# Two small tiles move into the constants and one tile grows by 64 bytes: every later tile gets another start address

## The chip, the core and the metric

The kernel runs on one core of a Trainium2 chip. TensorE (PE in the profile) multiplies matrices, VectorE (DVE), ScalarE (ACT) and GpSimd (POOL) work element by element, and SyncE (SP) issues most of the DMA transfers. The metric is the device time of one execution in microseconds. Before the change the median of three runs is 1049.33 us, the lowest 1048.02 and the highest 1049.53.

## The reference, cut to what matters

The reference is a two-layer encoder on a sequence of 512 positions with 1024 features, in float32. Layer 0 mixes positions with stick-breaking attention of 16 heads, layer 1 with a gated linear recurrence; each layer ends in an MLP of width 4096 with a squared ReLU, and a last RMS norm stands at the end.

```python
def reference(x, norm_mix, norm_mlp, ...):
    for layer in range(2):
        h = rms_norm(x, norm_mix[layer])
        y = stick_breaking_attention(h, ...) if layer == 0 else rglru_block(h, ...)
        x = x + y
        h = rms_norm(x, norm_mlp[layer])
        u = relu(h @ w1)
        x = x + (u * u) @ w2
    return rms_norm(x, norm_final)
```

Nearly all the arithmetic is in dense products of a 512 x 1024 activation with weight matrices.

## The kernel before, in words

**Matrix products.** A float32 operand is split into a high half and a low half of type fp32r (`xgh` and `xgl` for the activations, `wh` and `wl` for the weights), and a product is three matmuls: high with high, high with low, low with high (`three`, L217). Each matmul has a stationary operand of 128 x 128, loaded by a weight load ahead of it, and a moving operand of 128 rows by 512, 384 or 256 columns that is streamed past it. ScalarE makes the high halves with a cast, VectorE the low halves with a subtraction.

**The MLPs.** Each MLP (class `Mlp`, one object for each layer) goes through the 4096 hidden features in four quarters. Its products are done with a Strassen-like scheme of seven block products. In the *up* products (`up`, L966) a 256-column half of the activations moves past weights: blocks 0, 1, 2 and 6 take it from `xgh`/`xgl`, blocks 4 and 5 from the tile `s41` (in the profile `s`) and the tiles `low`, block 3 from spare columns of `bh`/`bl` and `low`. In the *down* products (`times`, L1061) 512 columns of weights (`wh`, `wl`) move past the hidden activations, which lie in `bh`/`bl` (the first unit of a quarter) or in `sh`/`sl` (the second). The recurrence of layer 1 and the output projections use `dense` (L219 to L221), where `xgh`/`xgl` or `bh`/`bl` move past weights.

**What sets the order.** TensorE's order is the order of the program text; the order on the other engines is set by a scheduler together with chains of instructions held in sequence. None of it is touched here.

**What sets the addresses.** A tile pool takes a stretch of the on-chip memory (224 KiB in each of 128 partitions, the same address in all), and pools opened later lie behind the earlier ones. Every tile's length is rounded up to 32 bytes. The first pool is `const` (L89), and its small tile `eps_t` takes 32 bytes, so that `xgh`, the next large tile, starts at 2592, which is 32 more than a multiple of 256. All pools behind it inherit such a start. In layer 1's MLP a pool `last` of one tile each of 4, 48 and 16 bytes (L1584, L1611, L1613, L1614) stands ahead of the MLP's pools, so that these lie 128 bytes further on than in layer 0. `ss` and `bias` hold row sums of squares for the last norm; `early` is one element that nobody reads, written to have a table of ScalarE loaded in time.

Of the kernel before, what the change touches and what calls it, by code (L numbers as in the profile page):

```python
# [11 lines left out]
F32 = mybir.dt.float32  # L12
F32R = mybir.dt.float32r
AF = mybir.ActivationFunctionType
# [3 lines left out]
P = 128  # L18
S = 512
D = 1024  # L20
C = D // P
# [3 lines left out]
EPS = 1e-6  # L25
RG_C = 8.0
SCALE = HD ** -0.5


START = [  # L30
# [31 lines left out]
def hybrid_encoder(  # L62
# [24 lines left out]
    V, A, G, PE = nc.vector, nc.scalar, nc.gpsimd, nc.tensor  # L87

    const = ctx.enter_context(tc.tile_pool(name="const", bufs=1))  # L89
# [26 lines left out]
    make_identity(nc, ident)  # L116
    eps_t = const.tile([P, 1], F32, tag="eps", name="eps_t")
    V.memset(eps_t, EPS)

    xgh = const.tile([P, C, S], F32R, tag="xgh", name="xgh")  # L120
    xgl = const.tile([P, C, S], F32R, tag="xgl", name="xgl")
# [19 lines left out]
    class Squares:  # L141


        def __init__(self):
            self.acc = work.tile([P, S], F32, tag="ssq", name="ssq", bufs=1)
            self.begun = False
# [132 lines left out]
    NB = S // P  # L279
    PAIRS = H // 2  # L280
    half = [slice(0, HD), slice(HD, P)]
    so, early = {}, {}
# [7 lines left out]
    with ExitStack() as actx:  # L290
# [18 lines left out]
        for i in range(2):  # L309
            both = []  # L310
            for nm in ("h", "l"):
                t = sp.tile([P, 2 * P], F32R, tag=f"last{nm}{i}", name=f"last{nm}{i}")
# [120 lines left out]
        def inverse():  # L433
# [9 lines left out]
            with tc.high_priority():  # L443
                norm["root"] = A.activation(rc, pc[:, :NB], AF.Sqrt, bias=eps_t, scale=1.0 / D)
                V.reciprocal(rc, rc)
                for t in range(NB):
                    ts = slice(t * P, (t + 1) * P)
                    V.tensor_scalar(diag[:, ts], ident, rc[:, t : t + 1], None, ALU.mult)
                V.tensor_scalar(rp, rc, SCALE, None, ALU.mult)
                V.tensor_scalar(rn, rc, -SCALE, None, ALU.mult)  # L450
            norm.update(rc=rc, rp=rp, rn=rn)
# [315 lines left out]
    class Mlp:  # L767
# [28 lines left out]
        def __init__(self, ctx, layer):  # L796
            self.layer, self.sq, self.first = layer, Squares(), None
            self.V, self.A = Ordered(V), Ordered(A)
            self.mp = ctx.enter_context(tc.tile_pool(name=f"mlp{layer}", bufs=2))
            self.c = [  # L800
                self.mp.tile([P, 2, S], F32, tag=f"c{i}", name=f"c{i}", bufs=1) for i in range(4)
            ]
            self.begun, self.a = set(), {}
            self.turns = count()
            self.blocks = ExitStack()
            self.bp = self.blocks.enter_context(tc.tile_pool(name=f"blocks{layer}", bufs=2))
            self.u, self.lows, self.s3, self.slots = {}, {}, [], None

            self.s41 = self.bp.tile([P, C // 2, S], F32R, tag="s41", name="s41", bufs=1)

        def y(self, t, h):

# [500 lines left out]
    with ExitStack() as mctx:  # L1313
        mlp = Mlp(mctx, 0)
# [4 lines left out]
        last = {}  # L1319
# [261 lines left out]


    with ExitStack() as mctx:
        lp = mctx.enter_context(tc.tile_pool(name="last", bufs=1))  # L1584
        mlp = Mlp(mctx, 1)

        def between(c):
# [20 lines left out]
                )  # L1608


        A.activation(lp.tile([P, 1], F32, tag="rt", name="early"), eps_t, AF.Sqrt)  # L1611

        ss = lp.tile([P, NB, 3], F32, tag="ss", name="ss")  # L1613
        bias = lp.tile([P, NB], F32, tag="bias", name="bias")  # L1614

        def square(t, h, i, cols=slice(0, S), end=False):

# [129 lines left out]
```

## Time and profile before

| | |
|---|---|
| median of 3 runs | 1049.33 us (1048.02 to 1049.53) |
| span of the profiled execution | 1047.9 us |
| TensorE matmuls | busy 1035.1 us, 5868 |
| VectorE | busy 863.1 us, 1147 instructions |
| ScalarE | busy 701.5 us, 1082 instructions |
| mean granted TensorE clock | 0.996 |

The profiled execution shows its span, from the first to the last instruction, and no other time of its own; the median lies 1.4 us above it, and that difference is taken here for what lies around a span. Matmuls overlap in the records: a matmul's own duration holds the time until its last column has left the array, so what one costs in a long stream is the distance from its start to the next one's start. That distance is read from the view in order of time, whose rows give a start in microseconds, a duration, the engine, the line, output<-inputs and the shape.

### The profile page before, as it was taken

The numbers are of one execution on the slowest core, as the hardware profiler recorded it, in microseconds if no ns is written. First come the engines' busy times: TensorE is split into PE (matmuls) and PEld (weight loads), VectorE is DVE, ScalarE is ACT, GpSimd is POOL, SyncE is SP. The second block draws the span as 40 slices with busy tenths as digits, with TensorE's granted clock in tenths as the row PEclk, the third lists the DMA queues.
The fourth block names the chain that finished last, engine by engine and source line by source line (L and its number), as shares of the span: only waits on it lengthen the run. The fifth ranks groups of instructions, "written<-read, shape, count | busy, mean of one in ns | idle before, by whom it ended". The sixth has DMA issues, their size and how long they took to land.

```text
span 1047.9 us, 15859 instructions
## 1 busy us (share of the span) xinstructions
PE 1035.1 (99%) x5868; PEld 902.8 (86%) x5868; DVE 863.1 (82%) x1147; ACT 701.5 (67%) x1082; POOL 179.2 (17%) x238
## 2 busy tenths in 40 slices
PE   8999999999999999999999999999999999999997
PEld 7888888888888988988988788888888988988986
DVE  7888787848788898898899799984789797897897
ACT  6767676836766773773775699964755773773775
POOL 2344344420000010010011121200000010010013
PEclk9999999999999999999999999999999999999999
DMA  6745354537536667567582483352345667567553
GB/s 225 204 137 141 101 149 104 153 109 274 149 80 190 181 139 204 165 140 207 164 208 81 109 214 112 91 221 93 88 86 173 174 142 206 158 139 204 145 125 101
DMA packets 52828, 159.41 MB, mean 152 GB/s; under 512 B 6672, under 2 KB 7952, under 8 KB 52752
## 3 DMA queue, kind: packets, MB, share of 16 engines
q1 hardware_dynamic: 41808, 120.13, 34.4%
q0 software_dynamic: 10368, 37.75, 20.9%
q8 instruction: 46, 0.75, 0.3%
q10 hardware_dynamic: 576, 0.52, 0.2%
q14 instruction: 30, 0.25, 0.1%
HBM read 137.41 MB, written 4.19 MB: 135 GB/s over the span
## 4 chain that ended last, share of the span: by engine, by line
PE 88%; DVE 5%; ACT 3%; issue 2%; DMA 2%; ACTq 0%; POOL 0%; DVEq 0%; POOLq 0%
PE ps_t L1061 14%; PE ps_acc L966 8%; PE ps_z L966 8%; PE ps_acc L1061 7%; PE ps_acc L219 5%; PE ps_acc L221 5%; PE ps_acc L220 5%; PE ps_o L966 5%; PE ps_z L1061 4%; PE ps_o L219 2%; PE ps_t L220 2%; PE ps_o L220 2%; PE ps_o L221 2%; PE ps_t L221 2%; PE ps_t L219 2%
## 5 line engine op out<-in xcount | busy, mean ns | idle before, releaser
L757 ACT CAST wh<-b 128x1024 fp32r<-128x1024 f32 x168 | 174.0, 1047 | 125.6 <-DVE b L757 76.7
L757 DVE TENSOR_TENSOR wl<-b,wh 128x1024 fp32r<-128x1024 f32 x168 | 203.8, 1221 | 50.5 <-ACT wh L757 50.1
L1043 POOL DMA_DIRECT2D b<-in_w_dn x40 | 35.0, 875 | 360.9 <-DVE b L757 204.6
L219 PE MATMUL ps_acc<-xgh,wh 128*128 128x512 f32 x192 | 78.5, 409 | 0.0
L221 PE MATMUL ps_acc<-xgl,wh 128*128 128x512 f32 x192 | 75.2, 392 | 0.0
L220 PE MATMUL ps_acc<-xgh,wl 128*128 128x512 f32 x192 | 75.1, 391 | 0.0
L581 DVE TENSOR_TENSOR_SCAN scan<-keep,later 128x128 f32<-128x128 f32 (+1 forms) x64 | 59.6, 933 | 18.8 <-ACT keep L571 10.9
L214 DVE TENSOR_TENSOR wl<-raw,wh 128x512 fp32r<-128x512 f32 (+2 forms) x70 | 60.9, 895 | 16.2 <-ACT wh L212 16.1
L757 ACT ACTIVATE u<-u 128x512 f32<-128x512 f32 x100 | 63.1, 632 | 6.5 <-DVE u L757 4.8
L212 ACT CAST wh<-raw 128x512 fp32r<-128x512 f32 (+2 forms) x70 | 50.8, 759 | 23.1 <-PE ps_acc L221 7.3
L1043 POOL DMA_DIRECT2D b<-in_w_up x24 | 20.8, 867 | 240.5 <-DVE b L757 72.1
L585 POOL TENSOR_TENSOR w<-w,scan 128x128 f32<-128x128 f32 (+1 forms) x64 | 51.9, 813 | 55.9 <-DVE scan L581 53.2
L757 DVE TENSOR_TENSOR b<-b,b 128x1024 f32<-128x1024 f32 x48 | 58.7, 1224 | 1.3
L757 DVE TENSOR_TENSOR u<-u 128x512 f32<-128x512 f32 (+1 forms) x92 | 54.9, 596 | 2.7 <-ACT u L757 1.1
L966 PE MATMUL ps_z<-xgh,wh 128*128 128x256 f32 x192 | 54.2, 282 | 0.0
L966 PE MATMUL ps_z<-xgh,wl 128*128 128x256 f32 x192 | 54.1, 282 | 0.0
L757 ACT CAST wh<-raw 128x1024 fp32r<-128x1024 f32 x46 | 47.9, 1045 | 9.3 <-PE ps_acc L1061 8.4
L966 PE MATMUL ps_acc<-low,wh 128*128 128x256 f32 x192 | 53.6, 279 | 0.0
L1061 PE MATMUL ps_t<-wl,sh 128*128 128x512 f32 x126 | 50.1, 398 | 0.0
L1061 PE MATMUL ps_t<-wh,sh 128*128 128x512 f32 x126 | 49.6, 394 | 0.0
L1061 PE MATMUL ps_t<-wh,sl 128*128 128x512 f32 x126 | 49.4, 392 | 0.0
L1061 PE MATMUL ps_t<-wh,bh 128*128 128x512 f32 x126 | 49.2, 391 | 0.0
(399 smaller groups left out, 3434.4 us busy)
## 6 DMA issues: line engine op xcount, KB each, us to landing
b<-in_w_dn SPq DMA_DIRECT2D x48, 512.0 KB, 4.5
b<-in_w_dn POOLq DMA_DIRECT2D x40, 512.0 KB, 5.5
b<-in_w_up SPq DMA_DIRECT2D x36, 512.0 KB, 4.6
b<-in_w_up POOLq DMA_DIRECT2D x24, 512.0 KB, 5.3
raw<-in_w_m SPq DMA_DIRECT2D x16, 512.0 KB, 4.1
raw<-in_w_dn SPq DMA_DIRECT2D x16, 512.0 KB, 4.7
raw<-in_w_in SPq DMA_DIRECT2D x16, 512.0 KB, 4.2
raw<-in_w_qk SPq DMA_DIRECT2D x12, 512.0 KB, 3.7
```

The costliest lines, as they stand in the source:

```text
L212: A.copy(wh[:, k, :], raw[:, k, :])
L214: V.tensor_tensor(wl[:, k, :], raw[:, k, :], f(wh[:, k, :]), ALU.subtract)
L219: PE.matmul(ps, wh, ah, start=start, stop=False)
L220: PE.matmul(ps, wl, ah, start=False, stop=False)
L221: PE.matmul(ps, wh, al, start=False, stop=stop)
L581: V.tensor_tensor_scan(sc[:, S - n : S][:, ::-1], keep[:, :n][:, ::-1], later[:, S - n :][:, ::-1], 1.0, ALU.mult, ALU.max,)
L585: G.tensor_tensor(wt, wt, sc[:, S - n + 1 : S + 1], ALU.mult)
L757: ins = getattr(self.e, name)(*args, **kwargs)
L966: PE.matmul(ps[:, i * HS : (i + 1) * HS], m, y, start=new and i == k == n == 0, stop=i == 1 and k == C // 2 - 1 and n == 2, skip_group_che ...
L1043: G.dma_start(out=unit[b].rearrange("p j n -> p (j n)"), in_=unit["src"](to), accum_op=ALU.add)
L1061: PE.matmul(ps, m, y[:, jj, cols], start=first and n == 0, stop=last and n == 2, skip_group_check=not new,)
```

## The change

The last layer's pool is dropped. `ss` and `bias` become tiles of `const`, right behind `eps_t` and ahead of `xgh`; they take 64 and 32 bytes, so `xgh` and everything behind it move by 96 bytes. The one-element write `early` now goes to the first column of the MLP's result tile `c[0]`, which is overwritten later. And `s41`, the first tile of the pool of an MLP's blocks, gets 16 more elements (64 bytes) at its end that nobody uses, so that the blocks of weights behind it and `sh`/`sl` move by another 64 bytes. All engines execute the same instructions in the same order on the same amounts of data; the single ScalarE instruction `early` has another output and waits for two more semaphores.

```diff
+ASIDE = 16
...
     eps_t = const.tile([P, 1], F32, tag="eps", name="eps_t")
     V.memset(eps_t, EPS)
+    ss = const.tile([P, S // P, 3], F32, tag="ss", name="ss")
+    bias = const.tile([P, S // P], F32, tag="bias", name="bias")
...
-            self.s41 = self.bp.tile([P, C // 2, S], F32R, tag="s41", name="s41", bufs=1)
+            t = self.bp.tile([P, C // 2 * S + ASIDE], F32R, tag="s41", name="s41", bufs=1)
+            self.s41 = t[:, : C // 2 * S].rearrange("p (k s) -> p k s", s=S)
...
-        lp = mctx.enter_context(tc.tile_pool(name="last", bufs=1))
         mlp = Mlp(mctx, 1)
...
-        A.activation(lp.tile([P, 1], F32, tag="rt", name="early"), eps_t, AF.Sqrt)
-
-        ss = lp.tile([P, NB, 3], F32, tag="ss", name="ss")
-        bias = lp.tile([P, NB], F32, tag="bias", name="bias")
+        A.activation(mlp.c[0][:, 0, :1], eps_t, AF.Sqrt)
```

The built programs tell where the operands lie. The table lists all 5596 fp32r matmuls by the start address of the moving and of the stationary operand, as the rest of a division by 256 bytes; the text calls this rest the *residue* of an operand.

| columns | moving, stationary (where) | matmuls | residues before | residues after |
|---|---|---|---|---|
| 512 | `xg`, `bh`/`bl` past `wh`/`wl`, or `wh`/`wl` past `bh`/`bl` | 2016 | 32, 32 | 128, 128 |
| 256 | `xg`, `bh`/`bl` past `wh`/`wl` (up products), weights of v past `xg` | 1644 | 32, 32 | 128, 128 |
| 256 | `s41`, `low` past `wh`/`wl` | 552 | 224, 32 | 64, 128 |
| 256 | layer 1: `s41` and one `low` past `wh`/`wl` | 216 | 96, 32 | 64, 128 |
| 512 | `wh`/`wl` past `sh`/`sl`, layer 0 | 336 | 32, 224 | 128, 128 |
| 512 and 256 | `wh`/`wl` past `sh`/`sl`, layer 1 | 330 and 12 | 32, 96 | 128, 128 |
| 512 | recurrence and end of attention, weights in other pools | 234 | 32, 224 | 128, 64 |
| 256 to 512 | attention scores and values | 224 | 224, 224 | 64, 64 |
| 256 | last block of attention values (`last`) | 32 | 64, 224 | 160, 64 |

So before the change every moving operand but `last` starts 32 bytes off a multiple of 64, and every stationary one does; after it all but those 32 start on a multiple of 64, and 4338 matmuls have both operands on a multiple of 128.

## The prediction

> **What bounds the kernel now.** I read the page first, then who waits for whom on TensorE, then the matmuls in order of time, then the busy time by stage.
>
> ```profile
> PE 1035.1 (99%) x5868; PEld 902.8 (86%) x5868; DVE 863.1 (82%) x1147; ACT 701.5 (67%) x1082; POOL 179.2 (17%) x238
> PEclk9999999999999999999999999999999999999999
> PE 88%; DVE 5%; ACT 3%; issue 2%; DMA 2%; ACTq 0%; POOL 0%; DVEq 0%; POOLq 0%
> ```
>
> ```profile
> PE ps_z L437 <- DVE ssq L422: 1.6, 1, 1.6
> PE ps_z L381 <- DVE eps_t L118: 1.1, 1, 1.1
> PE ps_z L966 <- ACT u L757: 1.0, 1, 1.0
> PE ps_t L220 <- DVE wl L757: 0.8, 1, 0.8
> ```
>
> TensorE is busy 99% of the span at full clock, 88% of the chain that ended last is its own, and the four longest waits it has for others add up to 4.5 us. So the time is the number of matmuls times the distance from one to the next, and the question is whether that distance depends on where operands lie.
>
> **What a matmul costs at which placement.** Each pair of rows is the first and the last of a stretch without a gap in which all matmuls have one shape and, but for the parts of the last pair that are named below, one placement.
>
> ```profile
> 250.38 0.39 PE L219 MATMUL ps_o<-xgh,wh 128*128 128x512 f32 x1
> ...
> 288.24 0.39 PE L221 MATMUL ps_z<-xgl,wh 128*128 128x512 f32 x1
> ```
>
> 512 columns, residues 32 and 32: 167 steps in 37.86 us, 226.7 ns each.
>
> ```profile
> 333.65 0.28 PE L966 MATMUL ps_acc<-xgl,wh 128*128 128x256 f32 x1
> ...
> 336.17 0.28 PE L966 MATMUL ps_acc<-xgl,wh 128*128 128x256 f32 x1
> ...
> 336.88 0.28 PE L966 MATMUL ps_acc<-low,wh 128*128 128x256 f32 x1
> ...
> 338.92 0.28 PE L966 MATMUL ps_acc<-low,wh 128*128 128x256 f32 x1
> ```
>
> 256 columns: at residues 32 and 32, 21 steps in 2.52 us, 120.0 ns each; at 224 and 32, 18 steps in 2.04 us, 113.3 ns each. Same shape, same kind of weights, half a microsecond apart, and 6.7 ns less.
>
> ```profile
> 322.46 0.39 PE L1061 MATMUL ps_t<-wh,sh 128*128 128x512 f32 x1
> ...
> 327.95 0.39 PE L1061 MATMUL ps_t<-wh,bh 128*128 128x512 f32 x1
> ...
> 791.65 0.40 PE L1061 MATMUL ps_t<-wh,sh 128*128 128x512 f32 x1
> ...
> 797.25 0.39 PE L1061 MATMUL ps_t<-wh,bh 128*128 128x512 f32 x1
> ...
> 805.67 0.28 PE L966 MATMUL ps_acc<-s,wh 128*128 128x256 f32 x1
> ...
> 808.38 0.28 PE L966 MATMUL ps_acc<-low,wh 128*128 128x256 f32 x1
> ```
>
> The same program lines in layer 0 and layer 1, which differ only in the 128 bytes of the pool `last`: the 24 `sh`/`sl` matmuls take 228.8 ns each in layer 0 (residues 32 and 224; 5.49 us) and 233.3 in layer 1 (32 and 96; 5.60 us); the 256-column stretch that took 113.3 ns in layer 0 takes 117.8 in layer 1 (23 steps in 2.71 us; `s` at residue 96, most `low` still at 224). The placement sets part of the distance.
>
> From 256 to 512 columns at one placement the distance grows by 106.7 ns, that is 0.417 ns for a column, so 512 columns need 213.3 and 256 need 106.7. What remains is a fixed part: 13.3 ns at residues 32 and 32, 6.7 at 224 and 32, 15.5 at 32 and 224, 20.0 at 32 and 96. The 6.7 is 16 columns, or 64 bytes of an operand's row, and the 13.3 is twice that. This looks like rows read in pieces of 64 bytes: an operand that starts in the middle of a piece touches one piece more than its length needs.
>
> **The change, part by part.**
>
> The tiles themselves. No instruction is added or removed. `early` keeps its place on ScalarE (0.19 us at 693.74) and waits for two semaphores more, GpSimd's and its own engine's:
>
> ```profile
> 693.74 0.19 ACT L1611 ACTIVATE early<-eps_t 128x1 f32<-128x1 f32 x1
> 681.51 0.92 POOL L1530 TENSOR_SCALAR aa<-d 128x512 f32<-128x512 f32 x1 [8.59 <-DVE d L757]
> ```
>
> GpSimd's last piece of work ahead of it ended at 682.4, 11 us earlier. Behind `early` on ScalarE stands a cast into `xgh`; if this cover were gone, that cast and the MLP's first matmuls would be late by the difference. I cost it at nothing.
>
> VectorE and ScalarE. Their tiles move too. The trace has one operation at several placements:
>
> ```profile
> L757 DVE TENSOR_TENSOR wl<-b,wh 128x1024 fp32r<-128x1024 f32 x168 | 203.8, 1221 | 50.5 <-ACT wh L757 50.1
> L757 DVE TENSOR_TENSOR b<-b,b 128x1024 f32<-128x1024 f32 x48 | 58.7, 1224 | 1.3
> L757 DVE TENSOR_TENSOR wl<-raw,wh 128x1024 fp32r<-128x1024 f32 x38 | 46.7, 1229 | 1.1 <-ACT wh L757 1.0
> ```
>
> `b` lies at residues 224 and 96, `raw` at 32, most of `wh` and `wl` at 32: 1221, 1224 and 1229 ns, within 0.7%. I take nothing for these engines.
>
> The one placement for both layers. The two dearest placements disappear: layer 1's 342 `sh`/`sl` matmuls go from 20.0 ns of fixed part to that of two equal residues (now 13.3), 342 x 6.7 = 2.3 us; layer 0's 336 from 15.5, 0.7 us; some 288 of layer 1's up products (two blocks in two units in three quarters, 24 each) from 117.8 to 113.3, 1.3 us. Together 4.3 us, and this much follows even if only the difference of the two residues counts, since everything else keeps its difference (64 - 128 is 224 - 32 less a whole 256). The quarters say the same: layer 0's second up product starts 77.94 us after its first, layer 1's third 78.68 after its second.
>
> ```profile
> 333.42 0.28 PE L966 MATMUL ps_acc<-xgh,wh 128*128 128x256 f32 x1
> ...
> 411.36 0.28 PE L966 MATMUL ps_acc<-xgh,wh 128*128 128x256 f32 x1
> ...
> 883.01 0.28 PE L966 MATMUL ps_acc<-xgh,wh 128*128 128x256 f32 x1
> ...
> 961.69 0.28 PE L966 MATMUL ps_acc<-xgh,wh 128*128 128x256 f32 x1
> ```
>
> The start on a multiple of 64. No fp32r matmul of the trace has both operands there, so its price is bounded. Upper end: the whole 13.3 ns goes (6.7 where only that is left). Lower end: nothing goes, or the fixed part rises to the largest one seen, 20.0. I take one piece of 64 bytes, 6.7 ns a matmul, which is the smallest step between the rows and the one by which the 113.3 and the 120.0 differ: 5596 x 6.67 = 37.3 us. With the 4.3 that is 41.6 us of TensorE's time.
>
> The rule in the Trainium skill, TensorE: Matmul & The Clock Gate, section "Wait — 56ns, not 53.3ns?", is that a warm stream of matmuls runs at its columns over 2.4 GHz plus a fixed 2.5 ns or so. The trace's 0.417 ns for a column agrees, its fixed 6.7 to 20 ns does not; by that rule some 10 ns could go from each matmul, an estimate of about 60 us of TensorE's time.
>
> What the other engines let through. The stages of the down products are the narrow ones:
>
> ```profile
> 360.00:411.00 51.00, 51.00 (x278) 44.07 (x278) 48.61 (x55) 30.48 (x39) 5.20 (x6) 1.00 0.69 182
> ...
> 575.00:690.00 115.00, 114.01 (x498) 93.04 (x497) 99.64 (x142) 100.31 (x138) 20.41 (x18) 1.00 0.46 124
> ...
> 860.00:882.00 22.00, 22.00 (x96) 17.70 (x95) 21.34 (x24) 9.77 (x11) 1.73 (x2) 1.00 0.72 209
> ```
>
> (Stretch, its length, then busy time and instructions of TensorE, weight loads, VectorE, ScalarE, GpSimd.) In the first, TensorE's 278 matmuls lose 1.85 us and come to 49.15, while VectorE has 48.61 of work and idles 2.4 us now, mostly behind ScalarE's casts (50.1 of the 50.5 us of idle time in the `wl` row). If half of that idle time stays, the stage ends at 49.8 and gives 1.2 instead of 1.85. There are seven such stages, 4.5 us given back. In the third, 0.64 us would bring TensorE to 21.36 and VectorE is at 21.34. The recurrence (second row) keeps 11 us of room. The start and the end of the kernel, where little is streamed, cost another 2.5. So 41.6 - 7 = 34.6 us come through. The span of 1047.9 with 1.4 around it is the median, 1049.3; 1049.3 - 34.6 = 1014.7, say 1015. What is late next is VectorE's subtraction into `wl` in the down stages.
>
> **The rivals.**
>
> *All of the fixed part goes.* For it: it is 16 or 32 columns, pieces of 64 bytes, and both operands are now aligned. Against it: the tiles `last` start on a multiple of 64 as moving operands (their stationary ones do not) and are no faster than others of 256 columns:
>
> ```profile
> 119.19 0.28 PE L629 MATMUL ps_o<-lasth,v 128*128 128x256 f32 x1
> 119.31 0.28 PE L630 MATMUL ps_o<-lastl,v 128*128 128x256 f32 x1
> 119.43 0.28 PE L478 MATMUL ps_acc<-wh,xgh 128*128 128x256 f32 x1
> ```
>
> Two of them take 0.24 us. Price: 5596 x 13.3 less 768 x 6.6 is 69.3, with the 4.3 73.6 us; VectorE's floors in the seven stages keep some 12 of it: 988. Chance 0.24.
>
> *Only the difference of residues counts.* Then 13.3 ns is what a change of weights costs, and only the 4.3 us come: 1045. For it: the two layers, at one and the same 32 bytes off, already differ by 6.7 ns. Against it: the fixed part comes in steps of 64 bytes of row. Chance 0.20.
>
> *Placement does nothing that counts.* A matmul reads its rows in small pieces of which all these starts are multiples, the layers differ for another reason, and the time stays within 0.2%, which is about what a measurement of this kernel can tell from no change. Chance 0.07. The Trainium skill, SBUF — State Buffer, section "Specifications (TRN2)", gives pieces of 16 bytes, by which this would hold, as every start is a multiple of 32 before and after; the 113.3 against 120.0 speaks against it.
>
> *Equal residues collide.* This is the one on the other side. If the moving and the stationary stream get in each other's way when both start at the same place of a 256-byte stretch, and the more so the more exactly they start together, then the 4338 matmuls at 128 and 128 rise to the dearest fixed part seen, 20.0: 4338 x 6.7 = 28.9 us, all of it paid, since TensorE bounds: 1078. It decides from the point at which the 256-column `xg` stretch takes more than 120 ns a step. For it: 224 and 32 is cheaper than 32 and 32. Against it: 32 and 96 is dearer than 32 and 32. Chance 0.13.
>
> **How the numbers follow.** One piece less at each matmul: 0.36, 1015 us, by itself 1005 to 1025 (what VectorE gives back). With 0.24 for 988, 0.20 for 1045, 0.07 for no change and 0.13 for 1078, faster by over 0.2% is 0.36 + 0.24 + 0.20, less a little for a 1045 that half fails: 0.79; same 0.08; slower 0.13. The range from 985 to 1049 leaves out the collision (0.13) and what of the cheapest case lies still lower (978 to 998 by itself, some 0.07).
>
> **What would show it.** In the view in order of time the 256-column `xg` stretch of an up product goes from 120.0 to about 113 ns a step and the 512-column stretch from 226.7 to about 220; a step of 107 and 213 would be the first rival, 120 and 226.7 unchanged the second. Layer 1's quarter should equal layer 0's. VectorE's busy time should stay at 863 us and its share rise to 85%, with waits of TensorE for `wl` in the down stages. I am wrong if the steps stay, or if they shrink and the waits take more than 7 us back.

## The result and the profile after

The changed kernel takes 1048.23 us in the median of 13 runs (1045.75 to 1049.71), the kernel before 1049.07 us beside it (1048.02 to 1051.06). The ratio of the two is 0.9981 with a 95% interval of 0.9972 to 0.9989: 2.0 us shorter, between 1.2 and 2.9; the two medians alone are 0.8 us apart. The forecast was 1015. The profiled execution took 1046.34 us, with a span of 1044.4, 3.5 less than before. It is one of the shorter ones: the median of the 13 spans is 1046.3. In the later runs of both kernels an execution takes 1.9 us more than its own span, where 1.4 was taken ahead of the prediction; the gain that was forecast does not rest on it.

From the page of the changed kernel, the engines and the chain that ended last:

```profile
PE 1030.6 (99%) x5868; PEld 901.4 (86%) x5868; DVE 862.3 (83%) x1147; ACT 701.5 (67%) x1082; POOL 180.4 (17%) x238
PE 84%; DVE 7%; ACT 4%; issue 3%; DMA 2%; POOL 0%; ACTq 0%; SPq 0%; DVEq 0%; POOLq 0%
```

TensorE is busy 4.5 us less and its part of the chain fell from 88% to 84%, while VectorE's rose from 5% to 7% and ScalarE's from 3% to 4%. VectorE's own work is unchanged.

The matmuls of the changed kernel in order of time, each pair being the first of a stretch and the first behind it or the last of it, at the places that the prediction read, and for the last pair one quarter later:

```profile
250.61 0.39 PE L222 MATMUL ps_o<-xgh,wh 128*128 128x512 f32 x1
...
288.46 0.39 PE L224 MATMUL ps_z<-xgl,wh 128*128 128x512 f32 x1
...
322.61 0.39 PE L1065 MATMUL ps_t<-wh,sh 128*128 128x512 f32 x1
...
328.05 0.39 PE L1065 MATMUL ps_t<-wh,bh 128*128 128x512 f32 x1
...
333.60 0.28 PE L970 MATMUL ps_acc<-xgh,wl 128*128 128x256 f32 x1
...
336.12 0.28 PE L970 MATMUL ps_acc<-xgh,wl 128*128 128x256 f32 x1
...
789.99 0.39 PE L1065 MATMUL ps_t<-wh,sh 128*128 128x512 f32 x1
...
795.43 0.39 PE L1065 MATMUL ps_t<-wh,bh 128*128 128x512 f32 x1
...
884.08 0.29 PE L970 MATMUL ps_acc<-s,wh 128*128 128x256 f32 x1
...
886.81 0.28 PE L970 MATMUL ps_acc<-bh,wh 128*128 128x256 f32 x1
```

512 columns at residues 128 and 128: 167 steps in 37.85 us, 226.7 ns, as at 32 and 32 before. 256 columns at 128 and 128: 21 steps in 2.52 us, 120.0 ns, as before. So the move of all these operands to multiples of 64 bought nothing. What did change are the streams that had another placement in the two layers: 24 `sh`/`sl` steps take 5.44 us in layer 0 and in layer 1, 226.7 ns each (228.8 and 233.3 before), and 24 steps of `s`/`low` in layer 1 take 2.73 us, 113.8 ns (117.8 at the same place before).

The starts of the up products show it by quarters (to be read with 333.49 for the first of layer 0):

```profile
411.38 0.28 PE L970 MATMUL ps_acc<-xgh,wh 128*128 128x256 f32 x1
...
489.25 0.28 PE L970 MATMUL ps_acc<-xgh,wh 128*128 128x256 f32 x1
...
800.87 0.28 PE L970 MATMUL ps_acc<-xgh,wh 128*128 128x256 f32 x1
...
881.20 0.28 PE L970 MATMUL ps_acc<-xgh,wh 128*128 128x256 f32 x1
...
959.07 0.28 PE L970 MATMUL ps_acc<-xgh,wh 128*128 128x256 f32 x1
```

Layer 1's second step is 959.07 - 881.20 = 77.87 us (78.68 before), the same as layer 0's 489.25 - 411.38 = 77.87. Its first step is 80.33, and before it was 883.01 - 802.79 = 80.22: there nothing came through. The waits of TensorE in the changed kernel from 735 us on (between 235 and 575 us none is long enough to be listed), and three places in order of time:

```profile
PE ps_z L970 <- ACT u L760: 1.2, 1, 1.2
PE ps_acc L970 <- ACT u L760: 0.4, 1, 0.4
PE ps_t L1065 <- DVE wl L760: 0.2, 1, 0.2
```

```profile
389.30 0.39 PE L1065 MATMUL ps_t<-wh,sh 128*128 128x512 f32 x1
389.70 0.50 PE L1065 MATMUL ps_t<-wl,sh 128*128 128x512 f32 x1
390.04 0.39 PE L1065 MATMUL ps_t<-wh,sl 128*128 128x512 f32 x1
...
806.39 0.28 PE L970 MATMUL ps_acc<-low,wh 128*128 128x256 f32 x1
807.05 0.38 PE L970 MATMUL ps_acc<-bh,wh 128*128 128x256 f32 x1 [0.38 <-ACT u L760]
...
858.99 0.39 PE L1065 MATMUL ps_t<-wh,sh 128*128 128x512 f32 x1
859.54 0.50 PE L1065 MATMUL ps_t<-wl,sh 128*128 128x512 f32 x1 [0.16 <-DVE wl L760]
```

The third place in the kernel before:

```profile
860.65 0.40 PE L1061 MATMUL ps_t<-wh,sh 128*128 128x512 f32 x1
860.89 0.50 PE L1061 MATMUL ps_t<-wl,sh 128*128 128x512 f32 x1
```

Each wait is short, some below what the view of waits lists, but each takes a few tenths. From the first row to the second it is 0.40 us at 389.30 (0.28 before, 0.23 without a wait) and 0.55 at 858.99 (0.24 before), where TensorE is ready too early for VectorE's `wl`; at 806.39 it is 0.66 (0.12 before), where it is ready too early for ScalarE's result.

To add all this up, the matmul rows of two profiles were put beside each other in program order and the distances from each start to the next subtracted. A distance of more than 30 ns over the columns at 2.4 GHz in either profile counts as a wait, the others as stream. For the two MLPs (235 to 575 us, and 735 us to the end):

| pair of profiles | streams, us | waits, us | sum, us |
|---|---|---|---|
| before to after | -4.3 | +1.7 | -2.6 |

Of the 4.3, 2.0 are layer 1's `sh`/`sl`, 0.7 layer 0's, 1.0 the `s`/`low` streams, 0.5 the `bh`/`bl` matmuls of the down products. 1.2 of the 1.7 us of waits lie between 802 and 960 us. Outside the MLPs the same sums give 0.2 us more before 235 us and 1.2 less in the recurrence, where two waits differ (588.46 and 589.72 before: 1.9 us for two distances; 0.7 now). These two places also differ, by up to 2.9 us, between profiles of kernels whose edits touch neither, and in the two further pairs with this same change, below, the recurrence differs by 0.0 and 0.1 us. So they are taken to be no part of the change.

### The profile page after: what moved, and what is told of

Its sections match the earlier page's. It is cut to its first block, busy times and chain, and to the rows that moved or that the text cites. A ratio compares the mean times of both kernels' runs of the same rounds, so it can differ in the third digit from the quotient of the medians.

```text
span 1044.4 us, 15859 instructions
## 1 busy us (share of the span) xinstructions
PE 1030.6 (99%) x5868; PEld 901.4 (86%) x5868; DVE 862.3 (83%) x1147; ACT 701.5 (67%) x1082; POOL 180.4 (17%) x238
## 4 chain that ended last, share of the span: by engine, by line
PE 84%; DVE 7%; ACT 4%; issue 3%; DMA 2%; POOL 0%; ACTq 0%; SPq 0%; DVEq 0%; POOLq 0%
PE ps_t L1065 13%; PE ps_acc L970 8%; PE ps_z L970 7%; PE ps_acc L1065 7%; PE ps_acc L222 4%; PE ps_acc L223 4%; PE ps_acc L224 4%; PE ps_o L970 4%; PE ps_z L1065 3%; DVE wl L760 2%; PE ps_o L222 2%; PE ps_t L223 2%; PE ps_t L224 2%; PE ps_t L222 2%; PE ps_o L223 2%
## 5 line engine op out<-in xcount | busy, mean ns | idle before, releaser
L760 DVE TENSOR_TENSOR wl<-b,wh 128x1024 fp32r<-128x1024 f32 x168 | 203.6, 1220 | 49.2 <-ACT wh L760 48.9
L760 DVE TENSOR_TENSOR b<-b,b 128x1024 f32<-128x1024 f32 x48 | 58.7, 1223 | 1.3
L1065 PE MATMUL ps_t<-wl,bh 128*128 128x512 f32 x126 | 49.1, 390 | 0.0
```

The source lines that it names most:

```text
L760: ins = getattr(self.e, name)(*args, **kwargs)
L1065: PE.matmul(ps, m, y[:, jj, cols], start=first and n == 0, stop=last and n == 2, skip_group_check=not new,)
```

## The experiments

**Streams alone.** Is it where the operands start, or how far apart? A kernel of nothing but streams of 36 matmuls in the pattern of `three`, with the moving and the stationary operand at chosen starts:

```python
for n, kind in ((512, "wide"), (256, "half")):
    for i in range(16):
        stream(f"{kind}_move_{L[i]}", n, 32 * i, 0)       # moving at 0, 32, 64, ... bytes
    for i in range(8):
        stream(f"{kind}_both_{L[i]}", n, 32 * i, 32 * i)  # both
    for i in range(8):
        stream(f"{kind}_stat_{L[i]}", n, 0, 32 * i)       # stationary
```

> This kernel computes nothing of the reference; it only streams fp32r matmuls, 36 in a row for each placement, with stationary operands at a fixed residue and moving operands at residues 0, 32, ... 480 (names move), both at the same residue 0 to 224 (both), moving at 0 and stationary at 0 to 224 (stat), and moving 4 or 16 bytes on (fine), for 512 and for 256 columns. Theory A (the distance depends on moving residue minus stationary residue alone): all eight 'both' streams take 226.7 and 120.0 ns a matmul; 'move' at 192 (that is 224 and 32) takes 113.3 at 256 columns, at 64 (96 and 32) 117.8; 'stat' at 192 (32 and 224) takes 228.9 at 512 columns and at 64 (32 and 96) 233.3; 'move' repeats itself after 256 bytes, and some differences not yet seen, such as 128, may be cheaper or dearer than all of these. Theory B (rows are read in pieces of 64 bytes and the start itself counts): 'both' at 0, 64, 128 and 192 is cheaper by 6.7 ns than at 32, 96, 160 and 224.

In the view in order of time each stream is one row, so the distance of two rows' starts is that of 36 matmuls and one change of the output bank:

```profile
35.68 8.57 PE L44 MATMUL wide_move_b<-mv,st 128*128 128x512 f32 x36
44.08 8.41 PE L44 MATMUL wide_move_c<-mv,st 128*128 128x512 f32 x36
52.34 8.57 PE L44 MATMUL wide_move_d<-mv,st 128*128 128x512 f32 x36
...
169.44 8.36 PE L44 MATMUL wide_both_b<-mv,st 128*128 128x512 f32 x36
177.63 8.36 PE L44 MATMUL wide_both_c<-mv,st 128*128 128x512 f32 x36
185.82 8.36 PE L44 MATMUL wide_both_d<-mv,st 128*128 128x512 f32 x36
...
382.66 4.47 PE L44 MATMUL half_both_b<-mv,st 128*128 128x256 f32 x36
386.97 4.47 PE L44 MATMUL half_both_c<-mv,st 128*128 128x256 f32 x36
```

Both at 32 take 8.19 us (`both_b`), both at 64 take 8.19 (`both_c`), and so do all eight: with equal residues the absolute start does not matter. Moving 32 ahead takes 8.40, 64 ahead 8.26. Inside the streams, with d for moving less stationary start mod 256 bytes, a 512-column matmul takes 226.7 ns at d = 0, 228.9 at 64, and 232.7 to 234.5 at 32, 96, 128, 160, 192 and 224; it repeats after 256 bytes, and the stationary side mirrors the moving one. 256 columns take 120.0 at d = 0 and 116.7 to 120.0 at the others, but at 192 either 113.3 or 117.8. This settles the kernel's rows: 32 past 224 before was d = 64 (228.8 in both), 32 past 96 was d = 192 (233.3 in both), `s`/`low` at 224 past 32 was 192 (113.3) and at 96 past 32 was 64 (117.8), and equal residues are 226.7 and 120.0 wherever they are.

**Without the padding.** The changed kernel without its 64 bytes: `sh`/`sl` fall back to d = 64, in both layers.

```diff
-ASIDE = 16
+ASIDE = 0
```

> The changed kernel without the 64 bytes behind s41: sh/sl lie at 64 instead of 128, with wh/wl at 128. Theory A: both layers' sh/sl matmuls take the 228.9 ns of layer 0 before instead of 226.7; 678 of them cost 1.5 us, so this is 0.5 to 1.5 us slower than the changed kernel and 0.5 to 2 us faster than the kernel before, whose layer 1 had the dearer placements; layer 1's s/low matmuls stay at 113.5. Theory B': the gain is not from placement but from run to run differences of waits at the start and between the layers: then this run cannot be told from the changed kernel, and sh/sl still take 226.7.

1047.83 us, 0.9991 (0.9982 to 0.9999) of the kernel before, which took 1048.8 us beside it. By the ratios that is 1.0 us more than the changed kernel, as expected, but the two intervals overlap. The distances decide. The 24 `sh`/`sl` steps again, in layer 0:

```profile
323.06 0.39 PE L1065 MATMUL ps_t<-wh,sh 128*128 128x512 f32 x1
...
328.55 0.39 PE L1065 MATMUL ps_t<-wh,bh 128*128 128x512 f32 x1
```

5.49 us, 228.8 ns a step, with both operands on a multiple of 64. All `sh`/`sl` together take 1.25 us more than with the padding. So of the 4.3 us the pool `last`, whose 128 bytes set the layers apart, is worth 3, the padding 1.25.

**All starts 32 bytes on.** One tile of 32 bytes ahead of `xgh` takes every large tile off the multiples of 64, with all differences kept.

```diff
+    const.tile([P, 8], F32, tag="aside", name="aside")
```

> The changed kernel with 32 unused bytes ahead of xgh: every difference of residues is that of the changed kernel, but no large tile starts on a multiple of 64 any more (160 and 160 instead of 128 and 128). Theory A: every stream takes what it takes in the changed kernel (226.7, 120.0, 113.5), and the time is the changed kernel's within 0.1%, 0.998 of the kernel before. Theory B: matmuls get dearer and the time is at or above that of the kernel before.

1047.5 us, 0.9986 (0.9978 to 0.9995); the streams differ from the changed kernel's by 0.2 us in sum. The absolute start is worth nothing in the whole kernel either. The profiled execution was the slowest of the twelve (1049.56 us), and in the MLPs it waits 2.3 us longer than the changed kernel's, most of it at one place:

```profile
830.51 0.51 PE L971 MATMUL ps_z<-bh,wh 128*128 128x256 f32 x1 [1.86 <-ACT u L761]
830.81 0.42 PE L971 MATMUL ps_z<-bh,wl 128*128 128x256 f32 x1
```

Behind this wait for ScalarE's `u`, of 1.2 us in the changed kernel, the granted clock is 0.50 for some 3 us and 256-column matmuls are 0.21 us apart. Since the streams agree and the twelve times do not show such a loss, it is taken for a difference between executions. It tells how far the waits of a single profile can be trusted.

**Differences made worse.** 128 bytes between `bl` and everything behind it, so that all products of `xg`, `bh` and `bl` with weights go from d = 0 to 128, still on multiples of 128:

```diff
+    const.tile([P, 32], F32, tag="aside", name="aside")
```

> The changed kernel with 128 unused bytes behind bl: xgh, xgl, bh and bl stay, all weights move by 128, so that moving and stationary operands lie 128 apart in 2016 matmuls of 512 columns and 1644 of 256. Theory A, priced by the streams measured alone (233.5 instead of 226.7 at 512 columns, 118.7 instead of 120.0 at 256; and 234 matmuls from 228.8 to 233.3): 13.7 - 2.1 + 1.1 = 12.7 us of TensorE's time, all paid since it bounds: about 1060 us, ratio to the kernel before 1.010. Rival C (TensorE's distances are not what sets the time, since the other engines' work has to fit beside it anyway): under 4 us more than the changed kernel.

1055.33 us, 1.0041 (1.0025 to 1.0058). The stretch that took 226.7 ns:

```profile
250.59 0.39 PE L224 MATMUL ps_o<-xgh,wl 128*128 128x512 f32 x1
...
289.15 0.40 PE L225 MATMUL ps_z<-xgl,wh 128*128 128x512 f32 x1
```

166 steps in 38.56 us, 232.3 ns. The streams take 10.1 us more than in the changed kernel, where 12.7 was forecast. The spans of the two profiled executions differ by 8.8 us, the times by 6.3 (from the two ratios, whose intervals leave 4 to 8), so the forecast ratio of 1.010 was missed and the rival's limit of 4 us was passed. The difference alone moves the time, and more than half of the loss on TensorE is paid. In layer 0's MLP the waits are 0.9 us shorter, since TensorE comes later to the halves that it waited for; in layer 1's they are 0.8 longer, with the clock halved for a while as in the run before.

**A cheaper difference for the up products.** Since 256 columns can take 113.3 ns at d = 192, the MLPs used `xg` 64 bytes lower against the weights.

```diff
-    xgh = const.tile([P, C, S], F32R, tag="xgh", name="xgh")
-    xgl = const.tile([P, C, S], F32R, tag="xgl", name="xgl")
+    def placed(name, more):
+        t = const.tile([P, C * S + more], F32R, tag=name, name=name)
+        return [t[:, o : o + C * S].rearrange("p (c s) -> p c s", s=S) for o in (ASIDE, 0)]
+
+    (xgh, uph), (xgl, upl) = placed("xgh", 4 * ASIDE), placed("xgl", ASIDE)
...
-                return xgh[:, c, ts], xgl[:, c, ts]
+                return uph[:, c, ts], upl[:, c, ts]
```

> The changed kernel with xgh and xgl lengthened, so that the MLPs use them 64 bytes lower than the attention and the recurrence do: moving less stationary residue is 192 instead of 0 for 1056 up matmuls of 256 columns and for 384 of 512 columns (the MLPs' first products). Theory A with the streams measured alone (113.3 instead of 120.0, 233.3 instead of 226.7): -7.0 + 2.5 = -4.5 us of TensorE's time against the changed kernel; if all comes through about 1043 us, ratio to the kernel before 0.994; if half is given back to waits as in the change itself, 0.996. If those streams fall into the other state that the same residues showed alone (117.8), -2.3 + 2.5: nothing gained. Rival C: no difference from the changed kernel.

1050.43 us, 0.9996 (0.9985 to 1.0006): no gain. The 512-column products went to 233.3 ns, and the up products took 117.2 to 118.0 in the mean instead of 113.3. The `s`/`low` streams, whose difference the edit leaves as it is, went from 114.1 and 115.8 ns to 117.3 and 118.0, so that the streams of the MLPs became 2.0 us longer than in the changed kernel.

**What picks 113.3 or 117.8.** Streams alone again, 72 matmuls of 256 columns at d = 192, made by the moving side 192 higher (`move`) or the stationary side 64 higher (`stat`), each behind another stream:

```python
lead = dict(wide=(512, 0, 0), half=(256, 0, 0), ahead=(256, 64, 0), odd=(256, 96, 0))
for i, (name, how) in enumerate(lead.items()):
    for kind, rm, rs in (("move", 192, 0), ("stat", 0, 64)):
        stream(f"lead_{L[i]}", *how)
        stream(f"{name}_then_{kind}", 256, rm, rs, reps=24)
```

> This kernel computes nothing of the reference. Streams of 72 matmuls of 256 columns at residues 192 and 0 (move) and at 0 and 64 (stat), each right behind 36 matmuls of another placement; then streams of 384 columns at differences 0, 64, 128 and 192. If the two values seen for one difference (113.3 and 117.8) are two states of which the start of the stream picks one, the value changes with what ran ahead, and both placements show both values. If it is the placement itself (residue 0 and 64 is not 192 and 0), 'move' always takes 113.3 and 'stat' always 117.8.

```profile
36.30 8.64 PE L44 MATMUL wide_then_move<-mv,st 128*128 128x256 f32 x72
44.78 8.32 PE L44 MATMUL lead_a<-mv,st 128*128 128x512 f32 x36
...
65.75 8.34 PE L44 MATMUL half_then_move<-mv,st 128*128 128x256 f32 x72
73.92 4.46 PE L44 MATMUL lead_b<-mv,st 128*128 128x256 f32 x36
```

The very same 72 matmuls take 8.48 us behind 512-column ones and 8.17 behind 256-column ones at d = 0, 117.8 and, once settled, 113.3 ns each. Behind 256-column ones at d = 64 or 96 `move` takes 8.48 again. `stat` takes 8.48 behind the first two and 8.17 and 8.18 behind these. One difference has two states; what runs ahead picks one, and it lasts. (384 columns took 173.4, 173.3, 175.9 and 176.8 ns at d = 0, 64, 128 and 192.)

**Why half came back: VectorE's sums left out.** TensorE's streams became 4.3 us shorter and the MLPs 2.6. If the rest went to waits for VectorE, it must come through when VectorE has less to do. The same edit in the kernel before and in the changed one:

```diff
             if far or name in self.FAR:
                 G.dma_start(
                     out=unit[b].rearrange("p j n -> p (j n)"), in_=unit["src"](to), accum_op=ALU.add
                 )
-            elif to:
-                self.V.tensor_tensor(unit[b], unit[b], unit[to], ALU.add)
```

> The kernel before, with VectorE's 48 sums of weight blocks (the b<-b,b group, 48 x 1.224 us = 58.7 us of VectorE in the two MLPs) left out; the products that would use those sums then use the plain block, so this part of the computation is wrong and only the time is read. It is one half of a pair with the run that follows. Theory A (placement gives TensorE 4.2 us, and in the MLPs it then waits for halves of weights that VectorE is late with, which gives half back): this kernel is itself only 0 to 2 us faster than the kernel before, since before TensorE waits for VectorE little, and its own small waits of about 1 us in the MLPs go. Theory B (the 2.0 us that are missing have nothing to do with VectorE): the same here, 0 to 1 us; the two theories part in the next run.

> The changed kernel with the same 48 sums left out (the same part of the computation wrong). Theory A: with 58.7 us less of work on VectorE its halves of weights are there in time, so the whole placement gain shows: 3.5 to 4.2 us below the run before this one, in place of the 2.0 us that the two full kernels are apart. Theory B (what comes back is waits for ScalarE's u at a quarter's start, or run-to-run waits elsewhere): the pair stays 1.5 to 2.5 us apart.

1047.75 us (0.9984, 0.9975 to 0.9993) and 1043.01 us (0.9937, 0.9924 to 0.9951): 4.7 us apart (4.9 by the ratios, 3.5 to 4.2 expected), against 2.0 with the sums. (The first of the two is 1.7 us below the kernel before, as theory A had it.) The distances say why: in the MLPs the streams of this pair differ by 4.7 us and the waits by 0.0; between 235 and 575 us and from 735 us on, the trace of the second kernel lists no wait of TensorE. The gain of the placement was whole all along, and VectorE's sums held about half of it back. Leaving them out takes work from VectorE and also a step out of the chain ahead of `wl`; this pair does not part the two, the sums on POOL below keep the step.

**More for TensorE to win.** With what the streams alone had shown, only the upper chunks of `xg` are put 192 bytes higher in the MLPs, so that their products follow 256-column ones with d = 0.

```diff
+    UP = 3 * ASIDE
+    def placed(name):
+        t = const.tile([P, C * S + 4 * ASIDE], F32R, tag=name, name=name)
+        return [t[:, o : o + C * S].rearrange("p (c s) -> p c s", s=S) for o in (0, UP)]
...
+        def __getitem__(self, at):
+            c = at[1].start if isinstance(at[1], slice) else at[1]
+            return (self.hi if c >= C // 2 else self.lo)[at]
```

> The changed kernel, with chunks 4 to 7 of x times the norm's gain kept 192 bytes higher by the MLPs (chunks 0 to 3 stay where they were; each of the two tiles has 256 bytes more, so everything behind keeps its residue). 576 of the 256-column products (P2 and P4) then stand at a difference of 192 and follow equal-residue 256-column streams (P7, P1); 192 of the 512-column ones stand at 192 as well. If the state of a stream is picked by what runs ahead of it, as in the streams measured alone (113.32 after a 256-column stream with equal residues, moving side 192 higher), the 576 gain 6.7 ns each = 3.8 us and the 192 lose 6.6 ns each = 1.3 us: 2.6 us less on TensorE than the changed kernel, of which 1 to 2.6 us show: 1045.6 to 1047.2 us beside 1048.2, a ratio to the kernel before of 0.9955 to 0.997. If waits between the streams let them fall to the other state (117.8), 576 x 2.2 = 1.3 us gained against 1.3 lost: no change from the changed kernel.

1048.61 us, 0.9999 (0.9989 to 1.0009). The 48 steps of upper chunks in an up product, and the waits for `wl` in the down products:

```profile
349.45 0.28 PE L987 MATMUL ps_z<-xgh,wh 128*128 128x256 f32 x1
...
354.89 0.28 PE L987 MATMUL ps_z<-xgh,wh 128*128 128x256 f32 x1
```

```profile
PE ps_t L1082 <- DVE wl L777: 1.2, 5, 0.3
```

113.3 ns a step, as hoped; the streams of the MLPs are 2.0 us shorter than in the changed kernel. But the waits there are 3.3 us longer, with five for `wl` where there was one. In these profiles TensorE's gain is not only lost: its waits cost more than it, which neither case of the expectation had. The same kernel with the sums left out:

> The kernel with the upper chunks of x 192 bytes higher, and VectorE's 48 sums of weight blocks (58.7 us) left out, so the products that use them are wrong and only the time is read. In the run of the former with the sums the MLPs' streams on TensorE became about 2.2 us shorter and its waits in the same stretches 3.4 us longer. Theory A (VectorE sets the pace there, and TensorE's gain turns into waits for it): without the sums the gain shows, 1.5 to 2.6 us below the changed kernel without the sums (1043.01): 1040.4 to 1041.5, a ratio of about 0.9915 to 0.9925 to the kernel before. Theory B (the waits come from the placement itself, or from the other engines' writing to the higher places): no lower than the changed kernel without the sums, 1043 to 1045.

1040.73 us, 0.9911 (0.9897 to 0.9925), 2.3 us below the changed kernel without the sums, with 2.7 us less of streams in the MLPs and no waits. Both placements pay in full as soon as VectorE is not late.

**The sum by DMA.** In a complete kernel, one more group of sums taken from VectorE: the second group of the down half's P6, whose `wl` is the one waited for at 389.3 us.

```diff
-            FARS = [("P6", 0)]
+            FARS = [("P6", 0), ("P6", 1)]
```

> The changed kernel, complete, with one more of the sums taken from VectorE: for the second group of the down half's P6 the DMA that loads the block adds it (as it does already for the first group), 8 x 1.224 = 9.8 us less on VectorE, 8 x 0.87 us more on POOL, 4 MB more to move. TensorE's small waits for wl in the down halves stand at this product (the wl needed at 389.3 us). Theory A: those waits go and a part of what came back shows: 0.5 to 1.5 us below the changed kernel, 1046.7 to 1047.7, a ratio of 0.9967 to 0.9976 to the kernel before. Against it: the DMA can start only when the product two steps ahead has its halves, some 5.6 us before they are needed, and such a transfer takes 5.6 us to land; if it is late, TensorE waits up to 1 us in each of 8 quarters: up to 1056.

> Both edits: upper chunks 192 bytes higher, and the DMA's sum for the second group of P6. Theory A: TensorE has 2.2 us less to do in the MLPs and VectorE 9.8 us less; 1 to 3 us below the changed kernel with the upper chunks higher alone (1048.6): 1045.6 to 1047.6, and no slower than the run before this one; a ratio of 0.996 to 0.998 to the kernel before. Theory B (waits come from elsewhere): within 1 us of 1048.6. If the transfer is late: as in the run before, above 1050.

1072.38 us (1.0218, 1.0203 to 1.0232) and 1073.26 us (1.0228, 1.0213 to 1.0242). Of the first, TensorE's two longest waits, one of them in order of time, and the granted clock (the eighth column) in a stretch behind it:

```profile
PE ps_t L1065 <- ACT wh L760: 8.9, 7, 1.4
PE ps_t L1065 <- DVE wl L760: 5.3, 7, 0.8
```

```profile
393.01 0.50 PE L1065 MATMUL ps_t<-wh,sh 128*128 128x512 f32 x1 [1.32 <-ACT wh L760]
394.27 0.80 PE L1065 MATMUL ps_t<-wl,sh 128*128 128x512 f32 x1 [0.76 <-DVE wl L760]
394.87 0.63 PE L1065 MATMUL ps_t<-wh,sl 128*128 128x512 f32 x1
395.30 0.63 PE L1065 MATMUL ps_t<-wh,sh 128*128 128x512 f32 x1
```

```profile
394.30:395.50 1.20, 1.20 (x3) 1.01 (x4) 1.20 (x2) 1.20 (x3) 0.87 (x1) 0.50 0.00 0
```

The transfer is late, the case that the expectation named as against it, but the price was put at up to 1 us a quarter. In this quarter it is 3.8 beside the changed kernel: 2.1 us of waiting, and behind it matmuls 427 ns apart at half the clock. Over the MLPs it is 23.9 us: 3.7 to 4.2 in the five quarters where the clock was halved, 2.6, 1.3 and 0.4 in the others. These two runs say nothing on VectorE.

**The sum on POOL.** POOL is nearly idle there (5.2 us of the 51 in the prediction's first stretch) and needs no transfer.

```diff
-            elif to:
-                self.V.tensor_tensor(unit[b], unit[b], unit[to], ALU.add)
+            elif to:
+                e = G if pool else self.V
+                e.tensor_tensor(unit[b], unit[b], unit[to], ALU.add)
...
-                if ahead > (5 if far else 2 if name == "P5" else what[0] == "up"):
+                pool = (*what[::2], name) == ("down", 1, "P6")
+                if ahead > (5 if far or pool else 2 if name == "P5" else what[0] == "up"):
```

> The changed kernel, complete, with the sum of weight blocks for the second group of the down half's P6 made by POOL instead of VectorE: 8 x 1.224 = 9.8 us less on VectorE. POOL's nearest rows are 128x512 sums of 1.29 to 1.7 us, so 2.6 to 3.4 us for one of 128x1024, which starts two steps (5.6 us) ahead of the halves that need it, where the DMA needed 0.87 + 5.6 us. Theory A (VectorE's load gives half of the gain back): the waits for wl of 0.1 to 0.5 us a quarter go, 0.5 to 1.5 us below the changed kernel: 1046.7 to 1047.7, a ratio of 0.9967 to 0.9976 to the kernel before. Theory B (VectorE's load does not matter in the complete kernel): within 0.4 us of the changed kernel. If POOL's sums slow VectorE beside them, or are late: slower than 1049.

> The same with the upper chunks of x 192 bytes higher in the MLPs, where TensorE has 2.2 us less to do. Theory A: more of it shows than without POOL's sums: 1 to 3 us below the 1048.6 of that kernel, 1045.6 to 1047.6, a ratio of 0.996 to 0.998. Theory B: within 1 us of 1048.6. Late or disturbed: above 1049.

1048.81 us (0.9994, 0.9982 to 1.0006) and 1049.24 us (1.0005, 0.9996 to 1.0014): neither shows a gain in the time, and the range of theory A was missed by both. By distances against the changed kernel, the first lost 1.1 us of waits in the later quarters, as theory A has it, and found a new one of 0.9 us in layer 0's first, where the sum came late; the 3.1 us wait at the start of attention of this profile (0.1 in the changed kernel's) lies ahead of all that the edit touches. In the MLPs the second is 1.2 us below the kernel with the upper chunks higher alone. VectorE paid something too, here its subtraction into `sl` and POOL's sum:

```profile
389.76 1.57 DVE L760 TENSOR_TENSOR sl<-u,sh 128x512 fp32r<-128x512 f32 x1
```

```profile
387.47 3.30 POOL L1052 TENSOR_TENSOR b<-b,b 128x1024 f32<-128x1024 f32 x1 [5.08 <-DVE wl L760]
```

The subtraction takes 0.68 us elsewhere and ended 0.56 us after POOL's sum did. The Trainium skill, SBUF — State Buffer, section "SBUF: two separate sides", has it that VectorE, when it reads two operands from SBUF, and GpSimd take one port in turn for a whole instruction; the row agrees to 0.12 us, by which 0.56 falls short of the whole 0.68.

**Seven sums on POOL, in both kernels.** The same without layer 0's first quarter:

```diff
+                pool = (*what[::2], name) == ("down", 1, "P6") and self.layer + what[1] > 0
```

> The kernel before, complete, with the sum for the second group of the down half's P6 made by POOL in seven of the eight quarters (not in layer 0's first). Before, TensorE waited little for VectorE, so by theory A (VectorE's load gives back half of the placement's gain) and by theory B (it does not) this is within 0.7 us of the kernel before, 1048.4 to 1049.8: the MLPs' stretches 0 to 0.6 us shorter.

> The changed kernel with the same seven sums on POOL. Theory A: 1.1 us of its waits in the MLPs go and none comes in layer 0's first quarter: 1.0 to 1.2 us below the changed kernel, near 1047.1, a ratio of 0.9965 to 0.9975 to the kernel before, and 2.5 to 3.5 us below the run before this one in the stretches of the MLPs, in place of 2.5 for the kernels without POOL's sums. Theory B: no lower than the changed kernel, a ratio of 0.998 to 0.999.

1050.05 us (1.0005, 0.9997 to 1.0014) and 1047.61 us (0.9981, 0.9972 to 0.9990). The first is within the 0.7 us of the kernel before that was expected, with 0.8 us less in the stretches of the MLPs (0 to 0.6 expected). In the time the second equals the changed kernel, and the ratio of 0.9965 to 0.9975 that theory A named was missed. In the stretches of the MLPs theory A did better: 1.6 us below the changed kernel (1.1 named), and 3.4 below the kernel before with the same edit (2.5 to 3.5 named). The whole profile is no shorter than the changed kernel's: 1.0 us of wait came back in the recurrence, which comes out differently from profile to profile, and 0.5 lie behind the last matmul. The four kernels with sums on POOL also take 2.4 us around their spans, in the mean, where the kernels before and after take 1.9; by the median of its spans the second is 1.3 us below the changed kernel (1045.0 and 1046.3), by the time it is not.

| pair of profiles | VectorE's load | streams of the MLPs, us | waits there, us | sum, us |
|---|---|---|---|---|
| before to after | all | -4.3 | +1.7 | -2.6 |
| the same, seven sums on POOL | 8.6 us less | -4.4 | +0.9 | -3.4 |
| the same, sums left out | 58.7 us less | -4.7 | 0.0 | -4.7 |
| changed kernel to upper chunks higher | all | -2.0 | +3.3 | +1.3 |
| the same, sums left out | 58.7 us less | -2.7 | 0.0 | -2.7 |

The less VectorE has to do, the more of one and the same gain on TensorE reaches the end of the MLPs. Each row compares single profiles, and after the 2.3 us of the run with all starts 32 bytes on, the rows of +1.7, +0.9 and +3.3 us of waits would prove little by themselves; the rows without the sums are borne out by the times (4.7 and 2.3 us). The streams' column grows a little too. In the changed kernel the 24 `s`/`low` steps from 809.9 us on, behind the wait at 807.05, took 117.8 ns each, where without the sums, and without that wait, they took 113.5. That the wait does it is not shown: with a wait there, two other profiles have 113.5 and 114.4. No complete kernel was measurably faster than the changed one.

## Why the prediction was wrong

**The step that failed: the start on a multiple of 64.** It priced "one piece of 64 bytes, 6.7 ns a matmul", at 5596 x 6.67 = 37.3 us. Measured: nothing. The 256-column stretch stayed at 120.0 ns and the 512-column one at 226.7 with both operands on a multiple of 128; the streams alone gave one value for all eight common starts, and 32 bytes more for every tile changed the time by no measurable amount. The reading behind it was that steps of 6.7 ns, 16 columns, mean rows read in pieces of 64 bytes. The steps are there, but they follow the distance between the two operands mod 256, and in the trace of before every row of the argument had both starts 32 bytes off a multiple of 64, so that it could not tell the two readings apart. The trace could have warned, for the steps were not all of 6.7 ns. At one and the same 32 bytes off the two layers differ by 4.5 ns (228.8 and 233.3, 113.3 and 117.8), not by the 6.7 that the prediction gives for its rival, and 13.3 and 15.5 differ by 2.2: neither is a whole number of pieces of 64 bytes.

**One placement for both layers** was priced at 4.3 us and is 4.3: layer 1's `sh`/`sl` 2.0 (2.3 forecast), layer 0's 0.7 (0.7), `s`/`low` 1.0 (1.3), and 0.5 in layer 1's `bh`/`bl` that was not named. What was named came to 3.7; that the sum is exact is luck. That these follow "even if only the difference of the two residues counts" was right, and layer 1's quarter now equals layer 0's.

**What the other engines let through** was put at 7 of 41.6 us: 4.5 as a share of VectorE's idle time in the down stages, and 2.5 for the start and the end, for which the prediction shows no row. The engine was right, as the pair without the sums shows, and the place (`wl` in the down halves) for 0.9 of the 1.7 us. The share was not: 1.7 of 4.3 us came back in these profiles, two fifths instead of a sixth. The estimate weighed busy and idle time of whole stages. In fact the queue of VectorE is late at single products, such as the one at 389.3 us, long before a stage is full. The waits for ScalarE's `u` in layer 1's first up product (0.7 of the 1.7 us, the larger part at 806.39) were not counted at all; they too are gone without VectorE's sums.

**Costed at nothing, and nothing:** `early` (the sums of distances from 690 to 735 us agree to 0.0 us), and VectorE's own operations, whose rows now have 1220 and 1223 ns for 1221 and 1224.

**The rivals.** The nearest was *only the difference of residues counts*, at 1045 with a chance of 0.20: its mechanism is shown by the streams alone, and by 128 bytes between operands that cost 10.1 us of streams. It was still some 3 us too low, for the reason just given. *All of the fixed part goes* and *equal residues collide* are refuted by the unchanged 226.7 and 120.0; *placement does nothing that counts* is refuted by the 228.8 and 233.3 that became 226.7. The pieces of 16 bytes that the prediction took from the Trainium skill, SBUF — State Buffer, section "Specifications (TRN2)", do not tell these streams apart: 16 bytes of difference took 231.7 ns where 0 took 226.7 and 64 took 228.9. The fixed 2.5 ns of the Trainium skill, TensorE: Matmul & The Clock Gate, section "Wait — 56ns, not 53.3ns?", did not appear at any placement tried: the least fixed part is 13.3 ns at 512 columns and 6.7 at 256. The time itself lies just inside the upper end of the range. That is luck: the range reached up to 1049 for the sake of the rivals, and the mechanism behind 1015 had no part in it. Whether it is "faster by over 0.2%" cannot be told: measured are 0.19% (0.11 to 0.28).

## What to carry to other kernels

A step in the trace that is a round number of columns or bytes is a clue, not a mechanism: before it is multiplied by thousands of matmuls, look for two rows that differ only in the supposed cause, and if the trace has none, let the bare alternative ("only the difference counts") keep most of the chance. With fp32r operands, give moving and stationary tiles equal starts mod 256 bytes where 512 columns are streamed, and keep repeated code at the same starts. Where a second engine is busy for 83% of the time, as here, count a small gain on the first as half gained until it is seen which single product that engine is late for.

## What was not expected of the hardware

- The distance of fp32r matmuls depends on the moving less the stationary start address mod 256 bytes: 226.7 to 234.5 ns at 512 columns in multiples of 32 bytes (236.7 at 4 bytes), 113.3 to 120.0 at 256. For 512 columns equal starts are the cheapest; for 256 they are among the dearest. Why the difference counts, no run here shows.
- At 256 columns and a difference of 192 there are two states, 113.3 and 117.8 ns. The matmuls ahead of a stream pick one, and it lasted, once settled, for the rest of the 72 that followed. Why is open.
- Two waits of 1.32 and 0.76 us in a row left TensorE at a granted clock of 0.50, with 512-column matmuls 427 ns apart for the next 3 us, so that this late transfer cost 3.8 us and not its 2.1. One wait of 1.86 us did the same in another run, one of 1.2 us in the changed kernel did not. The Trainium skill, TensorE: Matmul & The Clock Gate, section "Part 1: The HAM clock gate (the "warmup" mystery)", tells of a clock that halves after an idle window of about 3.4 us; here the idle time was shorter, and in the first case split by one matmul.
